# Expert weights read in 8 KB runs, and the scatter by ones in two float32r parts dealt over the next pair's steps

## The chip, the core and the metric

The kernel runs on one core of a Trainium2 chip. The metric is the device time of one execution in microseconds. Before the change three runs took 3477.11, 3481.97 and 3487.03 us; the median is 3481.97 us.

## What is computed

One layer of a diffusion backbone on 512 latent tokens of 2048 channels with a context of 256 tokens: a normed and modulated input, a wide input projection, two token mixers (a gated linear recurrence and a gated DeltaNet), a merge, an output projection, and then a mixture of 16 experts. The change lies in the last part, cut here to what matters:

```python
def expert_choice_ffn(h, router_w, w_gate, w_up, w_down):     # h: 512 tokens x 2048
    cap = max(1, (CAPACITY_FACTOR * n) // N_EXPERTS)           # 64 tokens an expert
    aff = softmax(h @ router_w)                                # 16 experts
    gate, idx = top_k(swapaxes(aff, 1, 2), cap)                # each expert chooses its 64 tokens
    xs = h[idx]                                                # gather
    a, u = xs @ w_gate[e], xs @ w_up[e]                        # 2048 -> 1024
    y = (silu(a) * u) @ w_down[e] * gate                       # 1024 -> 2048
    return zeros(n, d).at[idx].add(y)                          # scatter
```

The layer's output is x plus a per-channel gate times this, followed by one RMSNorm. Each of the 16 experts has three matrices of 2048 x 1024 float32 values, 8 MB each, 403 MB in all; each is read once.

## The kernel before

The program runs through stages: norm and modulation, the two mixers, the merge, the output projection (`project`), the choice of tokens (`route`), the experts (`experts`). On TensorE the order inside `experts` is the order in which the code stands (a manual schedule); the other engines' orders are set by a scheduler.

`prefetch` lists the weight tiles in the order of their use and puts each load on SP's queue. A tile is 1 MB: 128 partitions of 8 KB. A tile of `w_gate` or `w_up` holds two blocks of 128 rows, [128, 2, 1024], so that a partition reads two separate runs of 4 KB. A tile of `w_down` holds two blocks of 128 rows and 1024 columns, again two runs of 4 KB. Tiles go round 11 buffers (`EW`); the first 18 are loaded ahead, seven of them into buffers that later serve other uses (`aa`, `row5`, four `xo`, `xs`). Each later load waits on SP until the matmuls that read its buffer are done (L1161).

`experts` takes the experts in eight pairs, the two experts of a pair side by side in the two halves of the output partitions. For a pair:

- `begin` makes one-hot columns: `oh` (for the gather, times the tokens' norm) and `og` (for the scatter, times the routing gates).
- `gather` (four calls of 16 matmuls of x1 by `oh`, tile `px`, L1274) forms the experts' tokens by channel, `xs`; ScalarE applies the modulation (L1278). Two calls stand ahead of the pair's first step, two among its steps.
- Eight steps of gate (`pg`) and up (`pu`) products, each of 8 + 8 matmuls and four weight tiles (`pair`, L1289). After step k = 8 `og` is transposed and copied to `sct` (L1339 to L1341).
- The activation into `aa`, the next pair's `begin` and first two gathers, the transposes of the activation.
- The down products `py` in two blocks of 1024 columns, each of four steps of 8 matmuls. Behind each block comes its `scatter` (L1291): VectorE forms `y` from `py` and a row of the ffn's gate (L1296); then for two halves and four token tiles one float32 matmul of `sct` by `y` into `px` (L1299), and VectorE adds `px` to `xo` (L1300).

The last pair's down products come in blocks of 512, 512, 512, 256 and 256 columns, with tiles of four blocks of 128 rows (runs of 2 KB and 1 KB), and their scatters are put behind the next block's first step. At the end come the sums of squares, the final norm and four stores.

Of the kernel before, what the change touches and what calls it, by code (L numbers as in the profile page):

```python
# [17 lines left out]
D = 2048  # L18
# [5 lines left out]
E = 16  # L24
# [18 lines left out]
class Kern:  # L43
# [22 lines left out]

    pe = 0.0
# [13 lines left out]
    # ---------------------------------------------------------------- constants  # L81
    def consts(self):
        nc = self.nc
        cp = self.cp = self.pool("consts")
        tp = self.pool("ctmp", side="right")
        I = self.I

        def c(name, shape, dt=F32):
            return cp.tile(shape, dt, name=name)
# [4 lines left out]
        # silu of the conditioning vectors, rows p * 16 + k  # L94
# [24 lines left out]
        # masks of the levels inside a block of 32  # L119
# [14 lines left out]
        # pairs of neighbouring blocks of 16, parity of the block of 16  # L134
# [11 lines left out]
        # rows r and r +- 32 of 64; row r + 32  # L146
# [7 lines left out]
        # vectors as columns: ada_b of shift and scale, norm_mix, hgrn_norm, gdn_norm, hgrn_lb, conv  # L154
# [8 lines left out]
        nc.sync.dma_start(r1[96:112], r(I["norm_ffn"][0], 16))  # L163
# [12 lines left out]
        self.hg, self.gg, self.nffn = col[:, 48:56], col[:, 56:64], col[:, 96:112]  # L176
        self.conv = self.col[:, 1]
        # lower bound of the forget gate and one minus it, [dir * 8 + head]
# [163 lines left out]
    def dense(self, col, n=128, ctx=False, lat=True):  # L342
        """Channels col.. of the input projection, [channel, token]."""
# [90 lines left out]
    def hgrn(self, h, q, F, K, sga):  # L434
        """Slots of F, K: forward, backward; of Q: backward, forward."""
# [4 lines left out]
        # pairs of tokens inside a block of 32  # L440
# [18 lines left out]
        while b < 128:  # L459
# [20 lines left out]
            # K[s] of half s times the product over the other half; Q likewise  # L480
# [15 lines left out]
        # states before each chunk  # L496
# [41 lines left out]
        # both parts of the weights side by side, channels 0..31 and 32..63  # L538
# [29 lines left out]
        # softplus = max(x, 0) + log1p(u), u = exp(-|x|); log1p(u) = 2 atanh(u / (2 + u))  # L568
# [14 lines left out]
        # exp of any sum with a step below -110 is zero in float32 either way  # L583
# [45 lines left out]
    def gdn_in(self, h, R, free):  # L629
# [25 lines left out]
        def major(nm):  # L655
            """token major"""
# [54 lines left out]
    def gdn_solve(self, h, R, Z, free):  # L711
        """Decayed products and the inverse (1 + N)^-1 of every chunk; both directions."""
# [36 lines left out]
        # inverses of the diagonal blocks of 16  # L749
# [17 lines left out]
        for w in range(15, 0, -1):  # L767
            # forward: rows below w from row w; backward: the mirror image
# [10 lines left out]
        # blocks of 16 to blocks of 32  # L779
# [20 lines left out]
        # to blocks of 64  # L800
# [25 lines left out]
        # to the whole chunk  # L826
# [17 lines left out]
    def gdn_chain(self, h, d, R, Z, po, seen):  # L844
        """One direction; seen: products summed so far into each chunk of po."""
# [76 lines left out]
    def fill(self, jobs):  # L922
        """Products with split weights, a step of the contraction at a time; jobs: (column, end)."""
# [32 lines left out]
    def job_gate(self, n):  # L956
        """One of the merge gates, to DRAM."""
# [8 lines left out]
    def ada_block(self, i):  # L966
        """Columns 2 D + 512 i.. of the conditioning: gate of the mixer, shift, scale and gate of the ffn."""
# [19 lines left out]
        else:  # L987
            pr = self.px.tile([128, 4], F32, name="mx")
            for j in range(4):
                self.mm(pr[:, j:j + 1], acc[:, j * 128:j * 128 + 128], self.ones[:, 0:1])  # L990
# [20 lines left out]
    def merge(self):  # L1011
# [28 lines left out]
        self.close("sg")  # L1040

    def project(self):
        """x1 = x + gate * (m @ w_out), its sums of squares and the router's products."""
# [4 lines left out]
        # affinities of the tokens of tile 2 half + u, [token, u, half * 32 + expert]  # L1048
# [13 lines left out]
        nc.scalar.dma_start(rw, I["router_w"][0].rearrange("(k p) e -> p k e", p=128))  # L1062
# [15 lines left out]
        for nb, n in enumerate(widths):  # L1078
# [17 lines left out]
            for k in range(c0 // 128, (c0 + n) // 128):  # L1096
                pt = pp.tile([128, 512], F32, name="pt", bufs=2)
                for t in range(4):
                    self.tr(pt[:, t * 128:t * 128 + 128], x1[t][:, k * 128:k * 128 + 128])
# [7 lines left out]
        # logits, [token, expert]  # L1107
# [27 lines left out]
    def prefetch(self):  # L1135
        """The experts' weights in the order of their use, the first ones also in buffers that are not needed yet."""
        nc, I = self.nc, self.I
        sp = self.ex = self.pool("ex")
        wg = I["w_gate"][0].rearrange("e (k p) n -> e p k n", p=128)
        wu = I["w_up"][0].rearrange("e (k p) n -> e p k n", p=128)  # L1140
# [4 lines left out]
        def load(src):  # L1145
# [16 lines left out]
            return w  # L1162

        tiles = []
        for pr in range(E // 2):
            es = (2 * pr, 2 * pr + 1)
            for k in range(0, KT, 2):
                for w in (wg, wu):
                    tiles += [w[e][:, k:k + 2] for e in es]
            for ns in self.blocks(pr):  # L1170
                n = self.rows(ns)
                for f in range(0, 8, n):
                    tiles += [wd[e][:, f:f + n, ns] for e in es]
# [366 lines left out]
```

## Time and profile before

| | |
|---|---|
| three runs, us | 3477.11, 3481.97, 3487.03 |
| median, us | 3481.97 |
| span of the profiled execution, us (the profile has no other time for it) | 3490.3 |
| TensorE matmul busy | 3205.6 us, 92% |
| VectorE / ScalarE / GpSimd busy | 42% / 24% / 11% |
| mean granted TensorE clock | 0.959 |
| HBM read | 703.14 MB |

The profiled execution is 8.3 us longer than the median of the three runs. Differences worked out from its rows are taken off the median. TensorE's busy time counts a matmul from its start to a modelled end, so 92% is not 92% of the engine's peak. The page cuts the span into 40 slices of 87 us; the experts fill slices 29 to 40 (from about 2457 us on).

### The profile page before, as it was taken

What the parts mean: (1) busy time and instruction counts of PE and PEld (TensorE: products, weight loads), DVE (VectorE), ACT (ScalarE), POOL (GpSimd) and SP (SyncE); (2) the same over time, 40 slices, a digit from 0 to 9 for tenths busy, and PEclk for the clock granted to TensorE, in tenths of its full rate; (3) what the DMA queues carried; (4) which work ended last, traced back from release to release, by engine and by line L of the source; (5) the groups of instructions that cost most, each with busy time, mean ns of one, the idle gap of its engine ahead of it and who ended that gap; (6) DMA issues with size and microseconds to landing.
All of it is one profiled execution on the core that took longest, in us unless ns stands there. A gap on an engine that the chain in (4) does not pass through costs nothing. (4 is left out here: it accounts for less than half of the span.)

```text
span 3490.3 us, 52531 instructions
## 1 busy us (share of the span) xinstructions
PE 3205.6 (92%) x22034; PEld 2294.7 (66%) x22034; DVE 1462.1 (42%) x3052; ACT 841.8 (24%) x1529; POOL 371.5 (11%) x303
## 2 busy tenths in 40 slices
PE   7999999999999997777777899999799999999997
PEld 5678888888888876666666678788544444444443
DVE  5323476557555557666765444432310111111012
ACT  4222322222223233333333232222111000000102
POOL 0000000000000253222222211000000000000002
PEclk8999999999999998889988999999899999999999
DMA  9834375547454444333333354632789999999998
GB/s 294 239 110 129 87 221 153 155 132 222 137 161 132 122 129 116 93 99 93 96 89 81 81 160 137 210 95 70 304 350 400 409 409 409 409 409 409 409 409 299
DMA packets 505692, 738.87 MB, mean 212 GB/s; under 512 B 21979, under 2 KB 334531, under 8 KB 502511
## 3 DMA queue, kind: packets, MB, share of 16 engines
q1 hardware_dynamic: 475903, 688.10, 58.2%
q10 hardware_dynamic: 29552, 47.41, 4.0%
q8 instruction: 173, 2.83, 0.3%
q14 instruction: 64, 0.52, 0.0%
HBM read 703.14 MB, written 32.30 MB: 211 GB/s over the span
## 5 line engine op out<-in xcount | busy, mean ns | idle before, releaser
L74 PE MATMUL pl<-hlh,whi 128*128 128x512 f32 (+1 forms) x1552 | 646.3, 416 | 1.0 <-ACT vo L321 0.7
L74 PE MATMUL pl<-hlh,wlo 128*128 128x512 f32 x1536 | 618.8, 403 | 6.8 <-POOL wlo L339 4.5
L74 PE MATMUL pl<-hll,whi 128*128 128x512 f32 (+1 forms) x1552 | 622.2, 401 | 0.0
L337 ACT ACTIVATE whi<-wraw 128x1024 fp32r<-128x1024 f32 (+1 forms) x280 | 289.3, 1034 | 908.1 <-PE pcx L74 230.2
L339 DVE TENSOR_TENSOR wlo<-wraw,whi 128x1024 fp32r<-128x1024 f32 (+1 forms) x200 | 253.6, 1269 | 356.2 <-ACT whi L337 354.8
L74 PEld LDWEIGHTS pl<-hlh,whi 128*128 128x128 f32 (+1 forms) x1552 | 300.6, 194 | 61.4 <-issue 1.4
L74 PEld LDWEIGHTS pl<-hlh,wlo 128*128 128x128 f32 x1536 | 297.4, 194 | 53.7 <-POOL wlo L339 5.9
L74 PEld LDWEIGHTS pl<-hll,whi 128*128 128x128 f32 (+1 forms) x1552 | 300.4, 194 | 35.7
L74 PE MATMUL pu<-ew,xs 128*64 128x512 f32 x1000 | 248.1, 594 | 4.4 <-DMA ew<-in_w_up 4.4
L74 PE MATMUL pg<-ew,xs 128*64 128x512 f32 x992 | 241.8, 603 | 2.9 <-DMA ew<-in_w_gate 2.9
L339 POOL TENSOR_TENSOR wlo<-wraw,whi 128x1024 fp32r<-128x1024 f32 x80 | 199.5, 2495 | 391.3 <-ACT whi L337 379.3
L979 DVE SCALAR_TENSOR_TENSOR aacc<-awt,sc,aacc 128x512 f32<-128x512 f32 x256 | 196.1, 766 | 106.9 <-DMA awt<-in_ada_w 84.2
L74 PE MATMUL py<-ew,aa 128*64 128x512 f32 (+1 forms) x1056 | 227.1, 584 | 0.1
L1278 ACT ACTIVATE xs<-px,fcol,acol 128x128 f32<-128x128 f32 x128 | 48.1, 456 | 663.7 <-PE px L74 663.7
L74 PEld LDWEIGHTS pu<-ew,xs 128*64 128x64 f32 x1000 | 91.5, 137 | 142.7 <-issue 129.7
L74 PEld LDWEIGHTS py<-ew,aa 128*64 128x64 f32 x1056 | 90.0, 137 | 131.2 <-issue 120.3
L74 PEld LDWEIGHTS pg<-ew,xs 128*64 128x64 f32 x992 | 84.2, 138 | 131.8 <-issue 120.6
L74 PE MATMUL pcx<-hch,whi 128*128 128x256 f32 (+1 forms) x528 | 151.4, 287 | 0.0
L74 PE MATMUL pcx<-hcl,whi 128*128 128x256 f32 (+1 forms) x528 | 149.4, 283 | 0.0
L74 PE MATMUL pcx<-hch,wlo 128*128 128x256 f32 x512 | 146.2, 286 | 0.0
L442 POOL TENSOR_TENSOR tmp<-K 128x512 f32<-128x512 f32 x8 | 18.9, 2365 | 1147.2 <-DVE K L428 1147.2
L1296 DVE TENSOR_TENSOR y<-py,row 128x512 f32<-128x512 f32 (+1 forms) x33 | 21.0, 671 | 277.8 <-PE py L74 277.8
(449 smaller groups left out, 4829.3 us busy)
## 6 DMA issues: line engine op xcount, KB each, us to landing
ew<-in_w_up SPq DMA_DIRECT2D x125, 1024.0 KB
ew<-in_w_gate SPq DMA_DIRECT2D x124, 1024.0 KB
ew<-in_w_down SPq DMA_DIRECT2D x124, 1024.0 KB
wraw<-in_w_in SPq DMA_DIRECT2D x208, 512.0 KB
awt<-in_ada_w SPq DMA_DIRECT2D x128, 512.0 KB
aw<-in_ada_w SPq DMA_DIRECT2D x32, 1024.0 KB
big<-n_d SPq DMA_DIRECT2D x8, 1536.0 KB
wraw<-in_w_out SPq DMA_DIRECT2D x24, 512.0 KB
```

Of the source, the lines that this page charges most:

```text
L74: self.nc.tensor.matmul(out, lhsT, rhs, start=start, stop=stop, skip_group_check=True)
L337: nc.scalar.activation(hi[:, :n], raw[:, :n], AF.Copy)
L339: eng.tensor_tensor(lo[:, :n], raw[:, :n], hi[:, :n].bitcast(F32), op=OP.subtract)
L442: G.tensor_tensor(ks, K[:, 0, :NL], K[:, 1, :NL], op=OP.add)
L979: V.scalar_tensor_tensor(acc, w[:, k], self.sc[:, k0 + k, 0:1], acc, op0=OP.mult, op1=OP.add)
L1278: S.activation(xs[:, k], px[:, j], AF.Identity, scale=self.acol[:, k:k + 1], bias=self.bcol[:, k:k + 1])
L1296: V.tensor_tensor(y[:, :n], py, row5[:, cs], op=OP.mult)
```

## The change

1. The tiles of `w_gate` and `w_up` hold 256 consecutive rows, two for each partition: [128, 2048] in one run of 8 KB. So channel 2 p + i of a block of 256 lies in partition p, and every operand that is contracted with them follows: `chan` takes every other column of `x1` (gather, router), and `nffn`, `router_w` and the modulation's columns are laid out alike. `nffn` is loaded by a DMA of its own, in pairs of values (8 bytes).
2. The tiles of `w_down` hold one block of 128 rows and all 2048 columns, one run of 8 KB; the down products of a pair are one block with four accumulators (two `py`, two `pu`). The last pair's blocks are as before.
3. The scatter matrix `sct` holds ones (float32r); the gates move into `gs`, which is multiplied into `y`. `y` is split into two float32r parts, `yh` (ScalarE) and `yl` (VectorE), and each token tile takes two float32r matmuls.
4. The scatter of a pair is a list of 16 pieces (4 column blocks by 4 token tiles). `step` deals one out behind each gate or up step of the next pair; in the last pair two behind each step of the down products.
5. `og` is transposed after the last step, not after k = 8. Constants that only the early stages need lie in a pool that is closed before `project`.

The core of the diff:

```diff
+    def chan(ap, k):
+        return ap[:, k // 2 * 256 + k % 2:k // 2 * 256 + 256:2]
...
-        nc.sync.dma_start(r1[96:112], r(I["norm_ffn"][0], 16))
+        nc.sync.dma_start(self.nffn.rearrange("p (k i) -> p k i", i=2),
+                          I["norm_ffn"][0].rearrange("(k p i) -> p k i", p=128, i=2))
...
-        wg = I["w_gate"][0].rearrange("e (k p) n -> e p k n", p=128)
+        wg = I["w_gate"][0].rearrange("e (k p i) n -> e p k (i n)", p=128, i=2)
...
-            for k in range(0, KT, 2):
+            for k in range(KT // 2):
                 for w in (wg, wu):
-                    tiles += [w[e][:, k:k + 2] for e in es]
+                    tiles += [(w[e][:, k:k + 1], True) for e in es]
...
-        w = self.opt.get("lb", (512, 512, 512, 256, 256)) if pr == E // 2 - 1 else (1024, 1024)
+        w = self.opt.get("lb", (512, 512, 512, 256, 256)) if pr == E // 2 - 1 else (D,)
...
-        return 2 if ns.stop - ns.start == 1024 else 4
+        return 1 if ns.stop - ns.start == D else 4
...
-                    self.mm(px[:, j], x1[t][:, k * 128:k * 128 + 128], oh[:, t].rearrange("p e s -> p (e s)"),
+                    self.mm(px[:, j], self.chan(x1[t], k), oh[:, t].rearrange("p e s -> p (e s)"),
...
+        def scatter(pr, pys, b, ns, act):
...
+                V.scalar_tensor_tensor(y, py, X[pr][4], row5[:, cs], op0=OP.mult, op1=OP.mult)
...
+            def parts(i):
+                y, cs, n, _ = items[i]
+                yh = sp.tile([128, 512], F32R, name="yh", bufs=2)[:, :n]
+                S.activation(yh, y, AF.Copy)
+                yl = sp.tile([128, 512], F32R, name="yl", bufs=2)[:, :n]
+                V.tensor_tensor(yl, y, yh.bitcast(F32), op=OP.subtract)
+                items[i] += (yh, yl)
+            def tokens(i, t):
+                _, cs, n, b, yh, yl = items[i]
+                sct = X[pr][3][:, t * 128:t * 128 + 128]
+                pz = pp.tile([128, 512], F32, name="px")
+                self.mm(pz[:, :n], sct, yh, stop=False)
+                self.mm(pz[:, :n], sct, yl, start=False)
+                V.tensor_tensor(xo[t][:, cs], (x1 if pr == 0 else xo)[t][:, cs], pz[:, :n], op=OP.add)
...
+        def step(n=1):
+            while todo and n:
+                f, *a = todo.pop(0)
+                f(*a)
+                n -= f.__name__ == "tokens"
...
                 pair(pgt, xs, KT, k, 2)
+                step()
                 pair(put, xs, KT, k, 2)
+                step()
...
+            step(99)
+            pg = pp.tile([128, 512], F32, name="px")
+            for t in range(4):
+                self.tr(pg[:, t * 128:t * 128 + 128], og[:, t].rearrange("p e s -> p (e s)"))
+            gs = sp.tile([128, 1], F32, name="gs")
+            V.tensor_reduce(gs, pg, axis=AX.X, op=OP.add)
+            sct = sp.tile([128, 512], F32R, name="sct")
+            V.tensor_scalar(sct, pg, 0.0, None, op0=OP.is_gt)
```

The order on TensorE from the end of one middle pair to the start of the next, before. `py` are the down products, `px<-y,sct` the scatter, `pg` and `pu` the next pair's gate and up products:

```order
L74 MATMUL py<-ew,aa 64x512 x32
L74 MATMUL px<-y,sct 128x512 x8
L74 MATMUL py<-ew,aa 64x512 x32
L74 MATMUL px<-y,sct 128x512 x8
L74 MATMUL pg<-ew,xs 64x512 x8
L74 MATMUL pu<-ew,xs 64x512 x8
L74 MATMUL pg<-ew,xs 64x512 x8
```

The same place now, where the last down products write `py` and `pu` by turns, two of each for one expert and then two of each for the other:

```order
L80 MATMUL py<-ew,aa 64x512 x2
L80 MATMUL pu<-ew,aa 64x512 x2
L80 MATMUL pg<-ew,xs 64x512 x8
L80 MATMUL px<-yh,sct 128x512
L80 MATMUL px<-yl,sct 128x512
L80 MATMUL pu<-ew,xs 64x512 x8
L80 MATMUL px<-yh,sct 128x512
L80 MATMUL px<-yl,sct 128x512
L80 MATMUL pg<-ew,xs 64x512 x8
L80 MATMUL px<-yh,sct 128x512
L80 MATMUL px<-yl,sct 128x512
```

The 16 float32 matmuls behind the down products have become 32 float32r matmuls, two behind each step of the next pair.

VectorE in one late pair now, from the next pair's gates to the last of the deals (`aa` and `y` on the left of `<-` are the four column blocks of `y`):

```order
L1404 TENSOR_REDUCE gs<-px 128x1
L1406 TENSOR_SCALAR sct<-px 128x512
L1320 SCALAR_TENSOR_TENSOR aa<-py,gs,row_21821 128x512 x2
L1320 SCALAR_TENSOR_TENSOR y<-pu,gs,row_21821 128x512 x2
L1329 TENSOR_TENSOR yl<-aa,yh 128x512 x2
L1338 TENSOR_TENSOR xo<-xo,px 128x512 x4
L1329 TENSOR_TENSOR yl<-y,yh 128x512
L1338 TENSOR_TENSOR xo<-xo,px 128x512 x4
L1329 TENSOR_TENSOR yl<-y,yh 128x512
L1338 TENSOR_TENSOR xo<-xo,px 128x512 x7
L1411 TENSOR_TENSOR aa<-aa,pg 128x512 x2
L1412 TENSOR_TENSOR aa<-aa,pu 128x512 x2
```

Four products, four differences and the 16 adds now stand here; the 16th add comes behind the activation's four products.

## Rows read from the trace of the kernel before

**Rows 1.** The page's 40 slices of 87 us: GB/s moved.
```profile
GB/s 294 239 110 129 87 221 153 155 132 222 137 161 132 122 129 116 93 99 93 96 89 81 81 160 137 210 95 70 304 350 400 409 409 409 409 409 409 409 409 299
```

**Rows 2.** Busy time by stretch, a steady pair; columns in its first line.
```profile
core 0: us, PE busy (x) PEld busy (x) DVE busy (x) ACT busy (x) POOL busy (x), PEclk, DMA share, GB/s
2700.00:2725.00 25.00, 24.23 (x94) 9.12 (x92) 6.79 (x10) 0.00 (x0) 0.00 (x0) 1.00 1.03 409
```

**Rows 3.** DMA, 2700 to 3400 us: packets and rate, bytes a packet under.
```profile
DMA packets 74189, 286.34 MB, mean 409 GB/s; under 512 B 4366, under 2 KB 4366, under 8 KB 74157
```

**Rows 4.** Chain of waits, one pair, 2858 to 2983 us: start, length, what.
```profile
2890.47 3.77 PE px L74 x32
2894.24 3.63 PE pg L74 x16
2897.87 3.43 PE pu L74 x16
...
2906.60 18.32 DMA ew<-in_w_up
...
2938.21 13.98 PE py L74 x64
2952.19 0.68 DVE y L1296
...
2952.92 7.71 PE px L74 x16
2960.62 13.98 PE py L74 x64
```

**Rows 5.** TensorE in order of time, first pair: start, length, what.
```profile
2491.91 3.70 PE L74 MATMUL pg<-ew,xs 128*64 128x512 f32 x16
...
2563.12 1.12 PE L74 MATMUL px<-y,ident 4*128 4x512 f32 x2
...
2569.19 1.97 PE L79 MATMUL px<-ident,aa 128*128 128x128 f32 x8
```

**Rows 6.** Chain of waits: the second pair's first step.
```profile
2616.87 3.63 PE pg L74 x16
```

**Rows 7.** DMA, 15 to 20 us: packets and rate.
```profile
DMA packets 290, 2.11 MB, mean 423 GB/s; under 512 B 32, under 2 KB 32, under 8 KB 32
```

**Rows 8.** SP's queue in order of time, 0 to 40 us.
```profile
9.11 2.02 SPq L211 DMA_DIRECT2D x<-in_x  x4
```

**Rows 9.** DMA, 3420 to 3430 us: packets and rate.
```profile
DMA packets 1942, 3.86 MB, mean 386 GB/s; under 512 B 58, under 2 KB 58, under 8 KB 1941
```

**Rows 10.** Busy time by stretch, first pairs and end, columns as above.
```profile
2570.00:2575.00 5.00, 5.00 (x22) 2.25 (x21) 0.00 (x0) 1.19 (x2) 0.00 (x0) 0.73 0.49 197
2575.00:2580.00 5.00, 5.00 (x26) 2.08 (x24) 0.00 (x0) 0.00 (x0) 0.00 (x0) 1.00 0.64 232
2595.00:2600.00 5.00, 5.00 (x25) 1.96 (x23) 0.13 (x1) 0.00 (x0) 0.00 (x0) 1.00 0.69 243
2620.00:2625.00 5.00, 5.00 (x26) 2.03 (x23) 0.00 (x0) 0.00 (x0) 0.00 (x0) 1.00 0.70 245
...
3462.00:3464.00 2.00, 2.00 (x15) 0.88 (x15) 1.37 (x2) 1.54 (x5) 2.00 (x2) 1.00 0.13 35
```

**Rows 11.** TensorE, output projection: four float32r matmuls in a row.
```profile
2390.08 1.07 PE L74 MATMUL po<-whi,mh 128*128 128x512 f32 x4
```

**Rows 12.** Groups of instructions, 2700 to 3350 us: count, busy, mean ns, idle before.
```profile
L74 PEld LDWEIGHTS px<-oh,x 128*128 128x128 f32 x640 | 72.6, 192 | 12.2 <-issue 12.2
L1300 DVE TENSOR_TENSOR xo<-xo,px 128x512 f32<-128x512 f32 x92 | 63.3, 688 | 27.6 <-PE px L74 27.6
```

**Rows 13.** TensorE in order of time, the end.
```profile
3468.67 1.95 PE L74 MATMUL py<-ew,aa 128*64 128x256 f32 x16
3471.14 2.35 PE L74 MATMUL px<-y,sct 128*128 128x256 f32 x8 [0.53 <-DVE y L1296]
```

**Rows 14.** TensorE in order of time: one step, both experts' tiles named apart.
```profile
2513.10 0.59 PE L74 MATMUL pu<-ew,xs 128*64 128x512 f32 x1
2513.16 0.59 PE L74 MATMUL pu<-aa,xs 128*64 128x512 f32 x1
```

More of the change, by code (lines that the diff above doesn't have):

```diff
@@ L84, in consts @@
         cp = self.cp = self.pool("consts")
+        self.fcol = cp.tile([128, 2, 16], F32, name="fcol")
+        fp = self.pool("front")
         tp = self.pool("ctmp", side="right")
         I = self.I
+        late = ("ident", "both", "before", "iota64", "sel", "nffn")
         def c(name, shape, dt=F32):
-            return cp.tile(shape, dt, name=name)
+            return (cp if name in late else fp).tile(shape, dt, name=name)
         V = nc.vector
@@ L1040, in merge @@
         self.close("sg")
+        self.close("gc")
+        self.close("front")
     def project(self):
@@ L1143, in prefetch, with load @@
         nld = [0]
-        def load(src):
+        def load(t):
+            src, pair = t
             n = nld[0]
@@ L1161, in load @@
             nc.sync.dma_start(w, src)
-            return w
+            return w.rearrange("p k (i n) -> p (k i) n", i=2) if pair else w
         tiles = []
@@ L1172, in prefetch @@
                 for f in range(0, 8, n):
-                    tiles += [wd[e][:, f:f + n, ns] for e in es]
+                    tiles += [(wd[e][:, f:f + n, ns], False) for e in es]
         ahead = [load(t) for t in tiles[:self.EW + 7]]
@@ L1268, in gather @@
         def gather(pr, kc):
-            oh, _, xs = X[pr]
+            oh, _, xs = X[pr][:3]
             px = pp.tile([128, 4, 128], F32, name="px")
@@ L1289, in pair @@
                         self.mm(o[r], lhs[:, k, r], ws[i][:, j, u * c:u * c + c], start=(k == 0), stop=(k == n - 1))
-        def scatter(pr, pys, b, ns):
+        todo = []
+        def scatter(pr, pys, b, ns, act):
+            last = pr == E // 2 - 1
+            items = []
             for u, py in enumerate(pys):
@@ L1294, in scatter @@
                 cs = slice(ns.start + u * n, ns.start + u * n + n)
-                y = sp.tile([128, 512], F32, name="y", bufs=2)
-                V.tensor_tensor(y[:, :n], py, row5[:, cs], op=OP.mult)
-                for t in range(4):
-                    pz = pp.tile([128, 512], F32, name="px")
-                    self.mm(pz[:, :n], sct[:, t * 128:t * 128 + 128], y[:, :n])
-                    V.tensor_tensor(xo[t][:, cs], (x1 if pr == 0 else xo)[t][:, cs], pz[:, :n], op=OP.add)
-                    if pr == E // 2 - 1:
-                        S.activation(x1[t][:, cs], xo[t][:, cs], AF.Square, accum_out=ss[:, t, b + u:b + u + 1])
-                        G.tensor_tensor(x1[t][:, cs], xo[t][:, cs], fn[:, cs], op=OP.mult)
+                if not last and u < 2:
+                    y = act[:, u * 512:u * 512 + 512]
+                else:
+                    y = sp.tile([128, 512], F32, name="y", bufs=2)[:, :n]
@@ new lines, in tokens @@
+            def tokens(i, t):
[5 more added lines that the diff above has]
+                V.tensor_tensor(xo[t][:, cs], (x1 if pr == 0 else xo)[t][:, cs], pz[:, :n], op=OP.add)
+                if last:
+                    S.activation(x1[t][:, cs], xo[t][:, cs], AF.Square, accum_out=ss[:, t, b:b + 1])
+                    G.tensor_tensor(x1[t][:, cs], xo[t][:, cs], fn[:, cs], op=OP.mult)
@@ new lines, in scatter @@
+            m = len(items)
+            parts(0)
+            if m > 1:
+                parts(1)
+            for i in range(m):
+                for t in range(4):
+                    todo.append((tokens, i, t))
+                if i + 2 < m:
+                    todo.append((parts, i + 2))
+        def step(n=1):
[3 more added lines that the diff above has]
+                n -= f.__name__ == "tokens"
+            while todo and todo[0][0].__name__ == "parts":
+                f, *a = todo.pop(0)
+                f(*a)
@@ L1332, in experts @@
                 pair(pgt, xs, KT, k, 2)
+                step()
                 pair(put, xs, KT, k, 2)
+                step()
                 if k in (2, 6):
                     gather(pr, k // 4 + 2)
-                if k == 8:
-                    pg = pp.tile([128, 512], F32, name="px")
-                    for t in range(4):
-                        self.tr(pg[:, t * 128:t * 128 + 128], og[:, t].rearrange("p e s -> p (e s)"))
-                    sct = sp.tile([128, 512], F32, name="sct")
-                    S.activation(sct, pg, AF.Copy)
-                    if last:
-                        fn = sp.tile([128, D], F32, name="xs", bufs=2)
-                        spread(fn, r)
+                if last and k == 8:
+                    fn = sp.tile([128, D], F32, name="xs", bufs=2)
+                    spread(fn, r)
+            step(99)
[6 more added lines that the diff above has]
+            V.tensor_scalar(sct, pg, 0.0, None, op0=OP.is_gt)
+            X[pr] += (sct, gs)
             for u in range(2):
@@ L1371, in experts @@
                 w = ns.stop - ns.start
-                pys = [pp.tile([128, 512], F32, name="py")[:, :min(w, 512)] for _ in range(max(1, w // 512))]
+                pys = [pp.tile([128, 512], F32, name=("py", "pu")[u // 2])[:, :min(w, 512)]
+                       for u in range(max(1, w // 512))]
                 n = self.rows(ns)
@@ L1375, in experts @@
                     pair(pys, at, 8, f, n)
-                    if late:
-                        scatter(*late.pop())
-                if last and 0 < i < len(bl) - 1:
-                    late.append((pr, pys, b, ns))
-                else:
-                    scatter(pr, pys, b, ns)
+                    if last:
+                        step(2)
+                scatter(pr, pys, b, ns, act)
                 b += len(pys)
+        step(99)
         man.__exit__(None, None, None)
@@ L1414, in run @@
         self.gc = self.pool("gc")
-        self.fcol = self.gc.tile([128, 2, 16], F32, name="fcol")
         stop = opt.get("stop")
```

17 lines of the change are left out of this document (10 added, 7 removed).

## The prediction

> **What bounds the kernel now.** I read the page's slices first: the experts fill slices 29 to 40, and from slice 32 on the bytes moved stand at 409 GB/s in every slice but the last [rows 1]. A number that stays so flat while the work goes through gathers, products and scatters is a limit of the transfers, not of the work. The stretch view agrees: DMA share 1.03, and TensorE at a granted clock of 1.00, its 2.4 GHz level [rows 2]. TensorE is 24.23 of 25 us "busy" there, so I checked how near it is to being the bound itself. The first pair answers that, for its weights lie ready: from its first step to the second pair's first step it takes 2616.87 - 2491.91 = 124.96 us, of which 6.07 (2563.12 to 2569.19) go to spreading a row, once only [rows 5, 6]. So TensorE alone needs 118.9 us a pair. The weights of a pair are 48 tiles of 1,048,576 bytes, at 409 GB/s [rows 3] 2.564 us each: 123.1 us. The later pairs repeat at that pace, and the chain of waits passes through a weight load in each of them [rows 4]. Transfers bind, and TensorE is only 4 us a pair behind them: whatever quickens the loads must also lighten TensorE.
>
> **The loads.** The 338 tiles behind the first 30 (18 loaded ahead, then the refills that wait for TensorE), up to the last pair's down tiles, change from two runs of 4 KB a partition to one of 8 KB. What does a packet of 8 KB cost? Near the start four loads of x are issued at 9.11 us [rows 8], 8 KB a partition, and while they land the rate is 423 GB/s [rows 7]: 2.479 us for 1 MB. That is a window of 5 us, so I test it by other rows. The last pair's down tiles, in runs of 2 KB, move at 386 GB/s [rows 9]. Over 16 engines a packet of 2048 bytes then takes 84.9 ns and one of 4096 bytes 160.2 ns: 75.3 ns for 2048 bytes more, and 9.6 ns that do not depend on the size. Carried on, 8192 bytes take 310.8 ns, or 421.7 GB/s. Two roads, one number; I take 423. Per tile 2.564 - 2.479 = 0.085 us, times 338 = 28.7 us, all on the path as long as the transfers bind. Bounds: 0 if the cost is not per packet, 28.7.
>
> The Trainium skill's page "DMA: Bandwidth & Descriptors" (Why small descriptors are slow) gives each packet about three cycles on top of one cycle for 32 bytes. By that rule 4 KB to 8 KB is worth 1.2%, some 10 us here by estimate; but 2 KB to 4 KB should then be worth 2.3%, and the trace shows 386 against 409, 6%. The measurement decides, and the rule stays as a rival.
>
> **The scatter on TensorE.** A block's scatter takes 8.43 us from the end of its products (2952.19) to the next products (2960.62), with the wait for `y` in it [rows 4]; two a pair: 16.9 us go. In come 16 deals of two float32r matmuls. Four such matmuls in a row take 1.07 us with 0.39 for the last, so 0.227 each [rows 11]; a deal is 0.45. A change between kinds of matmul costs some 0.2 (a step behind a gather takes 3.63, one behind a step 3.43 [rows 4]), so I count 0.65 a deal, 10.4 a pair (0.45 to 1.0 each: 7.2 to 16). I add 1.0 a pair because the next gather needs the bank of the 16th deal, whose add (0.69 us [rows 12]) stands on VectorE behind the activation's four products. And 1.7 for the new order of the down products: four matmuls of one expert, then four of the other. Both halves run at once now, starting 0.06 us apart though two matmuls of the first expert are queued ahead [rows 14]; with four ahead the second half starts up to two matmuls (four passes of 0.43) later. Sum 118.9 - 16.9 + 10.4 + 1.0 + 1.7 = 115.1 us a pair, under the 119.0 of the faster loads. TensorE waits about 4 us a pair, as before, so I see no reason for the clock to fall.
>
> **The first pairs.** While the second pair's first tiles are loaded the transfers wait for TensorE: 409 against 197 and 232 GB/s at 2570 to 2580 us (4.8 us lost), 243 at 2595 (2.0), 245 at 2620 (2.0) [rows 10]. The last two come from the first pair's scatters, which now move into the second pair: 4.0 us go. The first stays and grows, since some 13 loads (33 us) before it are each 0.085 faster: -1.1. Sum 2.9.
>
> **The end.** The last weights are in by about 3462.4 [rows 10], but TensorE ends its last down product at 3470.62 [rows 13], 8.2 us behind, for scatters stand between its products. With deals at 0.65 it keeps up; I expect 3 us behind, 5.2 gained. The split adds a copy and a difference of 256 columns (about 0.45 each) to the last chain before its matmuls, against shorter matmuls after: -1.0. Sum 4.2; bounds -2 to 7.
>
> **Edits at about nothing.** `yh` and `yl` are 4 copies and 4 differences of about 0.69 a pair on engines that stand idle over half the time [rows 2]. The later transposes of `og`, the sum `gs` and the comparison lie beside the 7 us of gathers. The first deal may wait for `yl`, which stands behind four products on VectorE (5 x 0.69 = 3.4 us, as long as the first step): 0 to 1 a pair, inside the 4 us. `nffn` in runs of 8 bytes puts 1024 small packets ahead of x: 1 us, 0 to 4. The scheduler interleaves the start a little differently, where transfers bind: 0, from -5 to 5. If the 4 us of slack are used up, each further us on TensorE costs 6 to 7 in all.
>
> **Sum.** 28.7 + 2.9 + 4.2 - 1.0 = 34.8 us. The profiled span is 3490.3, 8.3 above the median of the three runs; off the median: 3481.97 - 34.8 = 3447 us.
>
> **Rivals.**
> A cost by bytes or by loads, not by packets: the loads gain 0 to a third of the sum, 10 us, so 0 to 10 + 2.9 + 4.2 - 1.0 = 6 to 16, that is 3466 to 3476. For it: the window at 423 is short. Against it: the 2 KB rows.
> TensorE becomes the bound: deals at 1.0 us instead of 0.65 make 120.7 a pair, waits at the pair's turn one or two more. At 121.5 the six pairs after the first gain 1.6 each instead of 4.1: 15 us lost, 3462. The point is 119.0. Against it: each deal has 3.4 us until the next in which VectorE does one add of 0.69.
> Slower, by the gather: its weights are now every other column of x1, 8 bytes apart. Weight loads of 128 columns take 192 ns [rows 12], all from neighbouring columns; no row here has them apart. If they took twice as long, the 32 passes of a gather, now 3.77 us [rows 4], would take up to 7.5; four a pair add 15, and TensorE at 130 would bind: 6.8 us a pair over today's 123.1 for six pairs, 41, less about 5 gained at both ends: 3518. It decides as soon as a gather costs 1 us more, and it makes the kernel slower from 2 us more.
> The Trainium skill's page "SBUF — State Buffer" (Door 1: The DMA port swizzle) says that reads are at full rate with two hits in each line of 16 bytes, which two-word steps still have; no run here shows it.
> Slower, by the halves: if four matmuls of one expert in a row kept the other from running beside them, the down products would go from 28 to 55 us a pair and the whole to about 3590. Rows 14 speak against it: the second expert overtakes already.
>
> **Chances.** Forecast 0.73, a cost by bytes 0.10, TensorE the bound 0.06, gather 0.07, halves 0.04. A measurement of this kernel tells a difference over 0.3%, 10.4 us: faster means under 3471.5. The forecast and TensorE as bound lie there, and half of the cost by bytes: 0.84; its other half: 0.05; gather and halves: 0.11. Range for 8 in 10: the forecast's own bounds are 3436 (start 5 better, end 7) to 3458 (dearer deals, start 5 worse); I carry it on to 3470, over TensorE as bound and the lower part of the cost by bytes, and down to 3434 for the spread of the runs of 5 us.
>
> **What would show it.** Right: 420 to 424 GB/s in the slices from 2700 us on, packets of 8192 bytes, pairs 119 us apart, no scatter between the down products and the next step, a short wait for weights on TensorE each pair, and the last down product within 4 us of the last weights. Wrong in the loads: still 409, with TensorE waiting 8 us a pair. Wrong on TensorE: the rate falls below 420 with dips, SP waits longer, and the rows of `px<-oh` (gather), `px<-yh` (deals) or `py` (halves) are longer than above.

## The result and the profile after

| | before | after |
|---|---|---|
| runs, us | 3477.11, 3481.86, 3481.97, 3487.03 | 3429.75, 3441.93, 3442.90, 3444.52 |
| median, us | 3481.91 | 3442.41 |
| ratio, 95% interval | | 0.9879, 0.9858 to 0.9899 |
| span of the profiled execution, us | 3490.3 | 3440.1 |
| first gate product of the experts, us | 2491.91 | 2466.69 |
| from there to the end, us | 998.4 | 973.4 |

By the medians the kernel became 39.5 us faster; 34.8 was forecast. (The ratio in the table is not that of the medians, which is 0.9887: the run at 3429.75 us weighs in it.) The time is inside the range, but the table already holds a warning: the experts, where almost all of the forecast's sum lies, gained 25.0 us, and the stages ahead of them, for which the forecast counted -1 us, came 25 us earlier in these two executions.

First the flat row of the page's slices, the one that answers [rows 1]:

```profile
GB/s 305 235 118 124 89 216 148 165 139 201 150 160 143 123 129 119 87 98 103 96 89 82 89 138 147 175 151 68 293 330 420 420 420 420 420 420 420 420 418 300
```

It is as flat as before, at 420 instead of 409. The count of packets over the pairs, beside [rows 3]: all but about 4,000 small ones are now of 8192 bytes.

```profile
DMA packets 37462, 273.00 MB, mean 420 GB/s; under 512 B 4159, under 2 KB 4159, under 8 KB 4163
```

Busy time by stretch, the columns as in [rows 2, 10]: a steady pair, then four stretches that lie as far into the stage as those of [rows 10] did (it begins 25 us earlier now). The first two answer 197 and 232 GB/s, the last two 243 and 245.

```profile
2700.00:2725.00 25.00, 25.00 (x122) 11.38 (x120) 4.04 (x6) 2.14 (x5) 0.00 (x0) 1.00 1.01 419
2545.00:2550.00 5.00, 5.00 (x17) 2.41 (x18) 0.00 (x0) 1.41 (x3) 0.00 (x0) 0.73 0.21 87
2550.00:2555.00 5.00, 5.00 (x25) 1.99 (x23) 0.00 (x0) 0.00 (x0) 0.00 (x0) 1.00 0.65 223
2570.00:2575.00 5.00, 5.00 (x26) 2.05 (x24) 0.00 (x0) 0.00 (x0) 0.00 (x0) 1.00 1.01 419
2595.00:2600.00 5.00, 5.00 (x36) 3.66 (x36) 0.58 (x1) 1.51 (x4) 0.00 (x0) 1.00 1.01 419
```

The two dips of the first pair's scatters are gone. The gap ahead of them is still there and has grown, as was forecast: with 377 GB/s in the 5 us behind it, it costs 6.8 us where it cost 4.8.

The chain of waits in one pair (start, length, what), which answers [rows 4]:

```profile
2942.33 4.30 PE pg L80 x16
...
2959.66 0.66 PE px L80 x2
2960.33 3.63 PE pu L80 x16
2963.96 0.66 PE px L80 x2
2964.62 3.63 PE pg L80 x16
...
3013.32 7.82 PE px L80 x64
...
3037.62 16.38 DMA ew<-in_w_gate
```

Here the reader is to see a kernel with two bounds close together. Almost the whole chain is TensorE, yet a weight load stands in it here, and once more in the stage (16.90 us from 2796.59 us on). TensorE's waits over four pairs, 2820 to 3290 us (us in total, times, longest), say how thin the difference is:

```profile
PE px L85 <- ACT xs L1294: 4.6, 4, 1.2
PE px L80 <- DVE xo L1338: 1.4, 4, 0.3
PE pg L80 <- DMA ew<-in_w_gate: 0.4, 1, 0.4
```

The forecast had looked for a short wait for weights in each pair; there is one of 0.4 us in four. Here the bound by transfers hardly shows as waiting: small delays stretch the products instead (4.30 us for the step at 2942 us of the chain, 3.63 for the one at 2960). That it is the loads that stretch them, experiment 4 shows: with a third of the loads left out, all 73 steps that the trace shows unbroken between 2700 and 3280 us take 3.7 us on TensorE, while in the changed kernel 15 of 66 take 4.2 to 5.2.

The end, in place of [rows 13]: the stretch in which the transfers run dry, and the last down product and deal in TensorE's order of time.

```profile
3411.00:3413.00 2.00, 2.00 (x16) 1.21 (x16) 1.28 (x2) 0.83 (x3) 1.74 (x3) 1.00 0.34 109
3412.50:3413.00 0.50, 0.50 (x8) 0.35 (x6) 0.23 (x1) 0.50 (x3) 0.24 (x2) 1.00 0.10 31
```

```profile
3417.36 1.95 PE L80 MATMUL py<-ew,aa 128*64 128x256 f32 x16
...
3422.88 0.28 PE L80 MATMUL px<-yl,sct 128*128 128x256 f32 x1
```

The rate falls off slowly, and the last packet of weights is in at 3412.8; the last down product ends at 3419.3, 6.5 us later. Before it was 8.0 by the same packets (3462.6 to 3470.6).

### The profile page after: what moved, and what is told of

Read it like the earlier page. It is cut to its first block, busy times and chain, and to the rows that moved or that the text cites. A ratio compares the mean times of both kernels' runs of the same rounds, so it can differ in the third digit from the quotient of the medians.

```text
span 3440.1 us, 52591 instructions
## 1 busy us (share of the span) xinstructions
PE 3177.3 (92%) x22034; PEld 2295.7 (67%) x22034; DVE 1488.5 (43%) x3101; ACT 856.3 (25%) x1554; POOL 372.2 (11%) x303
## 5 line engine op out<-in xcount | busy, mean ns | idle before, releaser
L80 PE MATMUL pg<-ew,xs 128*64 128x512 f32 x992 | 248.9, 605 | 1.0 <-DMA ew<-in_w_gate 1.0
L1338 DVE TENSOR_TENSOR xo<-xo,px 128x512 f32<-128x512 f32 (+1 forms) x116 | 76.8, 668 | 362.5 <-PE px L80 362.5
L80 PE MATMUL pu<-ew,aa 128*64 128x512 f32 x448 | 199.4, 592 | 0.0
L80 PEld LDWEIGHTS pu<-ew,aa 128*64 128x64 f32 x448 | 61.4, 137 | 118.0 <-issue 118.0
```

The lines of the kernel that those rows point to most:

```text
L80: self.nc.tensor.matmul(out, lhsT, rhs, start=start, stop=stop, skip_group_check=True)
L1338: V.tensor_tensor(xo[t][:, cs], (x1 if pr == 0 else xo)[t][:, cs], pz[:, :n], op=OP.add)
```

## The experiments

The kernel before ran again beside each group of experiments. Its median was 3484.44 us beside 1 to 4, 3486.22 beside 5 to 8 and 3482.46 beside 9 to 12, against 3481.91 beside the changed kernel. So ratios compare between groups; medians of different groups do so to within some 4 us.

**1. The loads alone.** Runs of 8 KB and the new numbering; the scatter as it was, float32, behind the down products. The pools are closed early, as in the changed kernel.

```diff
-                self.mm(pz[:, :n], sct, yh, stop=False)
-                self.mm(pz[:, :n], sct, yl, start=False)
+                    self.mm(pz[:, :n], sct[:, t * 128:t * 128 + 128], y[:, :n])
...
-                step()
                 pair(put, xs, KT, k, 2)
-                step()
```

> Only the weights' runs of 8 KB and the new numbering of the channels; the scatter is as before, float32 matmuls right behind the down products. Theory (loads cost per packet, but without the lighter scatter TensorE needs about 119 to 122 us a pair): the rate in quiet stretches rises towards 420 GB/s, but TensorE becomes the longer of the two, so pairs take 120.5 to 122 us instead of 123.1 and the experts (first gate product to the end) 980 to 986 us against 998 before and 973 with both parts. Rival 'a cost by bytes, the scatter did the work': pairs stay at 123 and 409 GB/s. Rival 'loads alone': pairs of 119.8 and all of the 25 us. The stage ahead of the experts, which came 25 us earlier in the changed kernel: if that is caused by the code, this kernel has it too (experts start 10 us or more earlier than before); if it is chance of one execution, the median is 3482 less the experts' gain, 3465 to 3470.

Measured: 3449.72 us against 3484.44 before, ratio 0.9897 (0.9880 to 0.9913). The packets from 2700 to 3350 us, and two first steps of pairs in TensorE's order of time:

```profile
DMA packets 37379, 272.41 MB, mean 419 GB/s; under 512 B 4149, under 2 KB 4149, under 8 KB 4153
```

```profile
2836.74 3.70 PE L80 MATMUL pg<-ew,xs 128*64 128x512 f32 x16
...
2956.71 3.70 PE L80 MATMUL pg<-ew,xs 128*64 128x512 f32 x16
```

A pair takes 120.0 us, better than I had expected, and no more than in the changed kernel. The stage lasts 982.2 us, 16 less than before. So the loads carry most of the experts' gain (16 of 25 us), without the lighter scatter; in steady pairs the old scatter is just light enough.

**2. The scatter alone.** Runs of 4 KB, the old numbering, the pools closed early; the deals as in the changed kernel.

```diff
-        return ap[:, k // 2 * 256 + k % 2:k // 2 * 256 + 256:2]
+        return ap[:, k * 128:k * 128 + 128]
...
-        wg = I["w_gate"][0].rearrange("e (k p i) n -> e p k (i n)", p=128, i=2)
+        wg = I["w_gate"][0].rearrange("e (k p) n -> e p k n", p=128)
```

> Only the scatter by ones in two float32r parts, dealt out, and the closing of the early pools; weights in runs of 4 KB and channels numbered as before, norm_ffn taken from the transposed rows as before. Theory: the rate stays at 409 GB/s, a pair stays at 123 us with TensorE waiting 5 us in each, and only the first pairs and the end gain (5 to 9 us in the experts: 989 to 993 against 998). Rival 'the scatter did the work': pairs under 121 us and experts near 973. Gather matmuls are back at 3.77 us for 32 passes if the step of 8 bytes made the 3.97 of the changed kernel. Median 3482 less 5 to 9, and less up to 14 more if the earlier stages gain by the closing of the pools.

Measured: 3468.11 us, ratio 0.9957 (0.9944 to 0.9970); the stage 991.5 us, 7 less than before. The packets and a step that waits for its weights:

```profile
DMA packets 68881, 265.87 MB, mean 409 GB/s; under 512 B 4051, under 2 KB 4051, under 8 KB 68851
```

```profile
2950.80 3.65 PE L80 MATMUL pg<-ew,xs 128*64 128x512 f32 x12 [0.63 <-DMA ew<-in_w_gate]
```

The rate is back at 409 though the scatter is the new one: the rate belongs to the runs' length.

**3. The pools alone.** The kernel before, with the constants that only early stages need in a pool that is closed before the output projection.

```diff
+        fp = self.pool("front")
...
+        self.close("gc")
+        self.close("front")
```

> The kernel before with nothing but the constants split into a pool that is closed before the output projection (and gc with it), so that buffers behind it lie elsewhere; norm_ffn copied from the transposed rows. If the stages ahead of the experts gain by where the buffers lie and when they come free: experts start 5 to 25 us earlier and the median is 3457 to 3477. If that gain is chance of the one profiled execution or comes from norm_ffn's new load: 3482, ratio 1.000 within 0.002.

Measured: 3475.90 us, ratio 0.9977 (0.9967 to 0.9986): 8.5 us, all but 1.4 of them ahead of the experts (they last 997.0). Where? In the merge ScalarE rounds a chunk of weights, `whi`, for every 24 matmuls. First the kernel before (its second execution), then this one; start, length, what, idle time before it:

```profile
2111.74 1.06 ACT L337 ACTIVATE whi<-wraw 128x1024 fp32r<-128x1024 f32 x1 [2.58 <-PE pb L74]
2117.34 1.06 ACT L337 ACTIVATE whi<-wraw 128x1024 fp32r<-128x1024 f32 x1 [4.54 <-PE pb L74]
```

```profile
2110.83 1.06 ACT L343 ACTIVATE whi<-wraw 128x1024 fp32r<-128x1024 f32 x1 [4.38 <-PE pb L74]
2116.27 1.06 ACT L343 ACTIVATE whi<-wraw 128x1024 fp32r<-128x1024 f32 x1 [2.43 <-PE pb L74]
```

The same 24 matmuls take 5.60 us in both executions of the kernel before, and 5.44 in this kernel and in the five others compared, the changed one among them; the granted clock is 1.00 in either. 32 chunks make 5.1 us; from its first product to its last the merge takes 178.4 us here and took 183.1 and 182.9. TensorE, ScalarE, VectorE and GpSimd go through the merge in the same order in both, and only the places of the buffers differ; why the places matter was not tried. The rest lies mostly at the start: by 155 us the same instructions of VectorE and ScalarE come 4 us earlier here, and in experiment 2, than in the first execution of the kernel before, and 1.5 to 2 earlier than in the second.

**4. TensorE's own pair.** The changed kernel without the loads of `w_up`; the up products take the gate's tiles.

```diff
-                for w in (wg, wu):
+                for w in (wg,):
```

> The changed kernel without the loads of w_up: the up products take the gate's tile again, so what is computed is not the layer. 32 tiles a pair are loaded instead of 48 (80 us), so a pair lasts as long as TensorE's own work. The forecast had 115.1 us a pair; the trace of the changed kernel, where loads come in 119.8, suggests 117 to 118 (a deal of 0.87 us instead of 0.65). If deals cost what was forecast: 115. If loads, not TensorE, made the deals slow there: 113 to 115.

TensorE in order of time, one pair: its first step, deals, a gather, the first down products, and the next pair's first step.

```profile
2813.12 0.64 PE L80 MATMUL pg<-ew,xs 128*64 128x512 f32 x1
...
2818.36 0.50 PE L80 MATMUL px<-yh,sct 128*128 128x512 f32 x1
...
2819.01 3.70 PE L80 MATMUL pu<-ew,xs 128*64 128x512 f32 x16
2822.65 0.50 PE L80 MATMUL px<-yh,sct 128*128 128x512 f32 x1
...
2827.61 3.70 PE L80 MATMUL pu<-ew,xs 128*64 128x512 f32 x16
2831.25 0.50 PE L80 MATMUL px<-yh,sct 128*128 128x512 f32 x1
2831.59 0.39 PE L80 MATMUL px<-yl,sct 128*128 128x512 f32 x1
2831.82 3.92 PE L80 MATMUL px<-oh,x 128*128 128x128 f32 x32
2835.67 3.71 PE L80 MATMUL pg<-ew,xs 128*64 128x512 f32 x16
...
2902.35 1.93 PE L80 MATMUL py<-ew,aa 128*64 128x512 f32 x4
2904.12 0.59 PE L80 MATMUL pu<-ew,aa 128*64 128x512 f32 x1
...
2930.72 0.64 PE L80 MATMUL pg<-ew,xs 128*64 128x512 f32 x1
```

117.60 us, in each of six pairs. Experiments 5 and 7 take it apart.

**5. Deals by twos, TensorE alone.**

```diff
-                step()
                 pair(put, xs, KT, k, 2, True)
-                step()
+                step(2)
```

> As the kernel without the loads of w_up (TensorE's own pair 117.6 us), but the deals come two at every second step instead of one at every step, so that half the changes between float32 and float32r matmuls go. If a change of kind costs about 0.2 us each way and two float32r matmuls 0.45: 8 fewer changes there and back, 114.3 us a pair. If a deal's 0.87 us is work and not change: 117.6, and more if two deals in a row wait for their banks.

```profile
2815.51 0.50 PE L80 MATMUL px<-yh,sct 128*128 128x512 f32 x1
...
2816.64 3.70 PE L80 MATMUL pg<-ew,xs 128*64 128x512 f32 x16
...
2823.71 0.50 PE L80 MATMUL px<-yh,sct 128*128 128x512 f32 x1
2824.05 0.39 PE L80 MATMUL px<-yl,sct 128*128 128x512 f32 x1
2824.28 0.40 PE L80 MATMUL px<-yh,sct 128*128 128x512 f32 x1
2824.51 0.40 PE L80 MATMUL px<-yl,sct 128*128 128x512 f32 x1
2825.22 4.04 PE L80 MATMUL px<-oh,x 128*128 128x128 f32 x32 [0.31 <-DVE xo L1342]
```

A pair takes 115.7 us. Two steps with two deals in a row take 8.20 us (2815.51 to 2823.71); singly dealt they take 8.59, so a change of kind and back costs 0.39. Eight changes fewer would be 3.1 us; 1.9 came. Some of the rest goes where a gather stands behind a double deal and waits for its bank (the 0.31 above).

**6. Deals by twos in the whole kernel.** The same edit, with all weights loaded.

> The whole changed kernel with two deals at every second step. Theory (loads of 119.8 us a pair bind, TensorE is 2 us behind): even if TensorE gains 3 us a pair, pairs go from 120.5 to no less than 119.8: 0 to 5 us, median 3437 to 3443, no difference that can be told. Rival 'TensorE binds in the changed kernel': 3 us a pair for 6 pairs, 3424.

Measured: 3444.04 us, ratio 0.9877 (0.9861 to 0.9892), the changed kernel's 0.9879 over again. TensorE is 1.9 us a pair lighter and nothing is gained: pairs of 120.0 to 121.0 us, since 48 tiles at 420 GB/s take 119.8. The transfers bind in the changed kernel too.

**7. One matmul a deal, TensorE alone.**

```diff
-                self.mm(pz[:, :n], sct, yh, stop=False)
-                self.mm(pz[:, :n], sct, yl, start=False)
+                self.mm(pz[:, :n], sct, yh)
```

> Without the loads of w_up, and each deal with one float32r matmul (the small part yl left out) instead of two. If a deal is 0.45 us of work and 0.42 of change: 16 x 0.227 = 3.6 us less a pair, 114.0. If the second matmul costs more than its 0.227 (its weights are loaded again, or it waits for yl): 110 to 113.

A pair takes 114.1 us: 3.5 less, or 0.22 for the second matmul. So a deal is 0.44 of work and about 0.4 of change.

**8. The gains' load.** `norm_ffn` as rows, transposed, as before.

```diff
+        nc.sync.dma_start(r1[96:112], r(I["norm_ffn"][0], 16))
...
-        nc.sync.dma_start(self.nffn.rearrange("p (k i) -> p k i", i=2),
-                          I["norm_ffn"][0].rearrange("(k p i) -> p k i", p=128, i=2))
+        V.tensor_copy(self.nffn, col[:, 96:112])
```

> The changed kernel with norm_ffn taken as rows of 512 bytes and transposed, as before, so that its gains stand at the old numbering of the channels (the one part that is not computed as in the layer). The start ran 4 us earlier with the load of 8-byte pieces than without it (two kernels each). If that load is the cause: experts start 3 to 5 us later than in the changed kernel, median 3445 to 3447. If the cause is chance: 3442.

Measured: 3450.94 us, ratio 0.9904 (0.9888 to 0.9921), 8.5 us over the changed kernel and 6.9 over experiment 6, which ran beside it, but the intervals overlap. Its experts begin at 2474.9 us, with the pools' kernels (2475.7, 2475.9); the seven executions with the new load and the numbering by twos begin at 2463.1 to 2473.1. In order the engines differ only in the first 160 us and for a moment near 1390 us. More than the 3 to 5 us expected, in the direction expected; the size stays open. So does the cause. From 175 us on the same instructions of VectorE come 2.2 to 6.8 us earlier in the seven than in experiment 3, and 0.5 earlier in this kernel; in experiments 9 and 10, which load `norm_ffn` anew as well, but by fours, they come 0.8 to 1.0 later. At the start TensorE's order in those two is almost this kernel's and not the seven's, so what goes with the seven may be the scheduler's order and not the load itself.

**9. Numbered by fours.** Every fourth column of x1 instead of every second; loads still of 8 KB.

```diff
-        return ap[:, k // 2 * 256 + k % 2:k // 2 * 256 + 256:2]
+        return ap[:, k // 4 * 512 + k % 4:k // 4 * 512 + 512:4]
...
```

> The changed kernel with channels numbered by fours (every fourth column of x1, 16 bytes apart, instead of every second); the weights still come in runs of 8 KB. By the traces: steps of 8 bytes took the gather's weight loads from 192 to 196 ns and 32 passes from 3.77 to 3.85 us. Theory (the step does not matter to the weight load): 3.8 to 4.0 us again, pairs 120 to 121, median 3438 to 3447. Rival (words 16 bytes apart are read at half the rate): weight loads towards 390 ns, 32 passes 5 to 7.5 us, TensorE 123 to 132 us a pair, median 3460 to 3520. The Trainium skill's page 'SBUF — State Buffer' (Door 1: The DMA port swizzle) speaks for the rival: full rate needs two hits in a line of 16 bytes, and this step leaves one.

Measured: 3556.62 us, ratio 1.0211 (1.0197 to 1.0225), slower than the kernel before. Weight loads of the gather by group (count, busy, mean ns), first in the changed kernel, then here, and a gather in TensorE's order of time:

```profile
L80 PEld LDWEIGHTS px<-oh,x 128*128 128x128 f32 x640 | 77.3, 196 | 3.7 <-DVE xo L1338 2.9
```

```profile
L80 PEld LDWEIGHTS px<-oh,x 128*128 128x128 f32 x579 | 136.2, 329 | 4.8 <-DVE xo L1338 4.4
```

```profile
2757.44 7.50 PE L80 MATMUL px<-oh,x 128*128 128x128 f32 x32
```

329 ns instead of 196; 32 passes take 7.43 us (to the next step's start) instead of 3.85. Four a pair are 14.3 us, and pairs take 132.2 us instead of TensorE's own 117.6. This is the forecast's rival "slower, by the gather" with its very numbers (up to 7.5 a gather, TensorE at 130), one step further out. The Trainium skill's page "SBUF — State Buffer" (Door 1: The DMA port swizzle) says that full bandwidth needs at least two hits in a line of 16 bytes. Steps of 8 bytes have two (196 ns here, 192 without a step), steps of 16 have one (329 ns): the trace agrees on both sides.

**10. Runs of 16 KB.** Numbered by fours, tiles of 2 MB in 5 buffers in place of 11 of 1 MB.

```diff
-                w = (self.ew1 if n % self.EW < self.opt.get("e1", 4) else self.ew2).tile([128, D], F32, name="ew")
+                w = (self.ew1 if n % 5 < 2 else self.ew2).tile([128, 2 * D], F32, name="ew")
...
-        wd = I["w_down"][0].rearrange("e (k p) n -> e p k n", p=128)
+        wd = I["w_down"][0].rearrange("e (k p i) n -> e p k (i n)", p=128, i=2)
```

> Numbered by fours, and the weights of all pairs but the last down products in runs of 16 KB a partition, tiles of 2 MB in 5 buffers (in place of 11 of 1 MB); four steps of gate products, then four of up products. Theory (a fixed cost of 9.6 ns on each packet, as worked out from 386 and 409 GB/s; 8 KB came out at 420): 16 KB give 428 GB/s, 117.6 us a pair of 48 MB, which is TensorE's own 117.6: pairs 118 to 119.5, and 5 to 12 us less than the changed kernel, 3430 to 3438, if the coarser buffers cost nothing. Rival 'packets end at 8 KB or the rate has its ceiling at 420': pairs 120 to 121, 3440 to 3446. Rival 'five buffers are too few': the rate dips in each pair and pairs take 121 to 124, 3446 to 3465. If step 4 makes the gather slow, this run shows the same rows as the run before it.

Measured: 3619.78 us, ratio 1.0388 (1.0374 to 1.0402), slower, with pairs of 139 to 143 us. The gather is as slow as in the run before it, which alone makes 132; the rest goes with a rate that dips in each pair (72 GB/s below), as the rival "five buffers are too few" has it, though that was not tried apart. The rate itself can be read in the stretches in which the loads run:

```profile
2720.00:2730.00 10.00, 8.88 (x39) 6.66 (x40) 0.00 (x0) 2.59 (x6) 0.00 (x0) 1.00 0.17 72
2760.00:2770.00 10.00, 7.34 (x16) 2.16 (x18) 1.58 (x4) 0.00 (x0) 0.00 (x0) 0.66 1.01 428
```

428 GB/s, the number that 9.6 ns a packet gives (the other full stretches of 10 us from 2700 us on have 426 to 436; the loads are also twice as large as before). (In the second stretch TensorE waits for weights, and its granted clock falls to 0.66.)

**11 and 12. Both kernels once more**, for the stages ahead of the experts.

> The kernel before once more, for a second trace of the stages ahead of the experts. If the 25 us of the first comparison there are the code's: experts start at 2488 to 2494 us. If part of it was chance (the first trace was 8 us over the median): 2480 to 2486, so that the code's part is about 15.

> The changed kernel once more, for the same reason: experts start at 2463 to 2473 us, the span of the kernels that share its front, and the experts take 973 us again, within 1.

The experts began at 2489.6 and at 2472.4 us and lasted 998.6 and 971.6. 2489.6 looks like "all the code's", but this execution, too, took 8 us more than the kernel's median (3490.28 against 3482.46), so that it does not decide. The experts' 971.6 is 1.8 from the changed kernel's first execution, where 1 was expected; the end, TensorE behind the last weights by 4.7 us and not 6.5, makes that difference. So the experts gained 25.0 and 27.0 us in the two pairs of executions, and by the medians the stages ahead gained 39.5 less that, 12.5 to 14.5 us, not the 25 of the first two traces.

## Why the prediction was right, and where it was not

**What bounds the kernel: right.** The transfers, at a rate set by the length of the runs: 409 with 4 KB whatever the scatter (experiment 2), 419 to 420 with 8 KB whatever the scatter (experiment 1), 428 with 16 KB (experiment 10). The packets' law was the right mechanism: 9.6 ns and 37.7 ns for each 1024 bytes, drawn from 2 and 4 KB, gave 421.7 for 8 KB and gives 428.3 for 16 KB. By the rule of the Trainium skill's page "DMA: Bandwidth & Descriptors" (Why small descriptors are slow), about three cycles a packet, this step would be worth 1.2%, by estimate. The runs show 2.7% (420 against 409).

**The term of the loads: too large.** I took 423 GB/s from a window of 5 us over 421.7 from the packets; it is 420: 2.497 us a tile, and 338 x (2.564 - 2.497) = 22.6 us instead of 28.7. From the first gate product to the last packet of weights it was 970.7 us (2491.9 to 3462.6) and is 946.1 (2466.7 to 3412.8): 24.6 less, and 24.7 between the second executions.

**The first pairs: nearly right.** 24.6 - 22.6 leaves 2.0 us, where 2.9 were forecast, and the rows have them: the two dips (4.0 us) are gone, and the gap that stays has grown by 2.0 us, where 1.1 were forecast.

**TensorE: dearer than forecast, and it cost nothing.** 117.6 us a pair where 115.1 were forecast. The mis-sized term is above all the deal: between two steps it costs 0.87 us by the step's pitch in experiment 4 (4.30 against 3.43 without one [rows 4]), not 0.65. I had counted the change of kind once, and it is paid going and coming back. Beside a gather, where the change is paid anyway, a deal takes 0.57 (2831.25 to 2831.82). From a pair's first step to the end of its last deal it is 77.8 us in experiment 4 (2813.12 to 2890.90), and it was 64.1 in the second pair of the kernel before (2616.80 to 2681.47, less 0.6 for the transposes of `og`): 13.7 more, of which 1.6 belong to the next term and 0.2 to the gathers. So the 16 deals come to 11.9 us, where 10.4 were forecast.

The 1.7 us for the order of the down products were there: four products of one expert run alone (2902.35 to 2904.12), then both halves run side by side, and the other expert's last four end inside the next pair's first step, whose deal comes 5.24 us after the step's start (2813.12 to 2818.36) and not 3.64 like the next one's (2819.01 to 2822.65). Most of what is left is the gathers, 0.5 us longer in all. Since 117.6 is still under 119.8 no time hung on any of this (experiment 6). The margin was 2 us a pair, not 4.

**The end: hardly gained.** TensorE stays 6.5 us behind the last weights (4.7 in the second execution), where 3 were forecast and 8.0 were before; from the last down product to the end it is 20.8 us against 19.7, the 1.0 that was forecast for the split. The term is 0.4 (2.2 in the second execution), not 4.2. "With deals at 0.65 it keeps up" failed: there are two deals behind every step of the last down products, and TensorE is busy without a break from 3405 to 3419 us.

**The stages ahead: missed.** The experts gained 25.0 where 28.7 + 2.9 + 4.2 = 35.8 were forecast. Some 12 to 15 us came from ahead of them, where I had -1.0 for `nffn` and "0, from -5 to 5" for the start. Closing the pools is worth 8.5 (experiment 3), some 7 of it ahead of the experts and most of that in the merge. Then the wait for weights at the turn to the output projection fell; TensorE's waits from 2190 to 2300 us, first with the pools alone, then in the changed kernel:

```profile
PE po L74 <- ACT whi L343: 7.5, 2, 6.6
```

```profile
PE po L80 <- ACT whi L348: 3.4, 2, 2.5
```

4 us less, in every kernel with the new loads and in none without them. The router's rows and the first expert weights both come in fewer packets there; which of them it is was not told apart. How much of the 4 us reaches the experts is open too: the output projection's products take 207.5 to 207.7 us in the changed kernel against 211.2 to 212.5 without the new loads, but 210.7 to 211.0 in experiments 1, 4, 5 and 6. The last few microseconds go with the order at the start that came with the new load of `norm_ffn` (experiment 8) and are inside the spread of single executions, which was 10 us among seven with the same code there. If they are real, the load's term of -1.0 has the wrong sign.

So the forecast of 3447 against 3442 is a sum of one term 6 us too large, one 4 too large, one 1 too large, and some 15 us that were not looked for. What bounds the stage was foreseen; that the total came within 5 us is luck, for the errors cancel.

**By medians the parts add up, roughly.** Pools 8.5; the scatter 7.8 more (3475.90 to 3468.11); loads and numbering 25.7 more (3468.11 to 3442.41). That is 42.0 against 39.5, for the kernel before stood 2.5 us higher beside experiments 1 to 4. From the other side, the loads 26.2 over the pools (3475.90 to 3449.72) and then the scatter 7.3. The scatter's 7 to 8 lie mostly at the ends of the stage: against experiment 1 the first pair takes 108.7 us instead of 125.1, as its scatters move on, and the last one takes 11 more.

**The rivals.** A cost by bytes fell with experiments 1 and 2, TensorE as the bound with experiment 6, the halves with 28.4 us from a pair's first down product to the next pair's first step (2902.35 to 2930.72). The gather's weights 8 bytes apart cost 4 ns of 192, and 32 passes 3.85 us instead of 3.77: the cliff that this rival spoke of exists, and lies one doubling further.

## What to carry to other kernels

Lengthen the runs of a load as long as the rate rises, and draw the fixed cost of a packet from two lengths in the trace before trusting a short window. A renumbering that makes runs longer is paid for where the operand is read with a step: by twos it was free, by fours it cost 133 ns on each weight load and some three times the gain. And compare the stage that was changed apart from the whole: here some 12 to 15 of 39.5 us came from the stages ahead of it.

## What the runs showed of the hardware that was not expected

- Packets of 2, 4, 8 and 16 KB a partition: 386, 409, 420 and 428 GB/s; close to a fixed 9.6 ns a packet, which would give 421.7 for 8 KB.
- Float32 weight loads of 128 x 128: 192 ns from neighbouring columns, 196 ns by steps of 8 bytes, 329 ns by steps of 16.
- A float32r pair of matmuls between float32 steps costs 0.87 us: 0.44 of work, about 0.4 for the change there and back.
- The same float32r matmuls of the merge, in the same order, took 5.60 us for 24 or 5.44, with only the buffers' places changed.
